# Splitting the last two weight blocks of fourteen more down products, and moving a product and eight squares near the end

## The chip, the cores and the metric

The kernel runs on one core of one Trainium2 chip. The metric is the device time of one execution in microseconds; of several runs the median is taken. The five engines that the profile names are PE (matrix products), DVE (vector), ACT (scalar), POOL and SP; SP here only issues DMAs.

## The reference

One layer of a hybrid encoder: a mixing part (attention, convolution and a two-way recurrent scan), then a mixture of sixteen experts, then a final normalisation. The change lies in the experts and in the end:

```python
def expert_choice_ffn(h, w_router, w_gate, w_up, w_down):
    B, S, D = h.shape                                  # 1, 1024, 1024
    cap = CAPACITY_FACTOR * S // N_EXPERTS             # 128 rows for each of 16 experts
    aff = jax.nn.softmax((h @ w_router).astype(jnp.float32), axis=-1)
    gates, idx = lax.top_k(jnp.swapaxes(aff, 1, 2), cap)
    xe = jax.vmap(lambda hb, ib: hb[ib])(h, idx)
    hid = jax.nn.silu(jnp.einsum('becd,edf->becf', xe, w_gate)) * jnp.einsum('becd,edf->becf', xe, w_up)
    ye = jnp.einsum('becf,efd->becd', hid, w_down) * gates[..., None].astype(h.dtype)
    bidx = jnp.arange(B)[:, None, None]
    return jnp.zeros_like(h).at[bidx, idx].add(ye)

    x = x + expert_choice_ffn(rms_norm(x, norm_ffn_g[l]), w_router[l], w_e_gate[l], ...)
    return rms_norm(x, final_norm_g)
```

All matrices are 1024x1024 float32, three for each expert: 192 MB of weights that are read once.

## The kernel before

The mixing part ends at about 860 us of the span; what follows is the experts' stage. An expert has three products: gate and up (from its 128 gathered rows `xe`) and down (from `hid`, the product of the two). Each is a sum over eight blocks of the contraction, `KT` = 8; a block is 128 rows of a weight matrix, and its product with the 128 rows fills two halves of 512 columns.

**How a block is computed.** A block is split: ACT rounds the raw float32 block into `ewh` (L1350 for down, L1354 for gate and up), DVE subtracts that from the raw block into `ewl` (L1351, L1355). The stationary side is split in the same way into `xh`, `xl` (rows) or `fh`, `fl` (hid). Then `mm3` makes three products for each half: high by high (L329), low by high (L330), high by low (L331), so six matmuls for a block. A block can also be left whole: `parts` yields the raw block with no low half, and `product` makes one float32 matmul for each half of it (L1455), with the whole stationary block `fw` (L1446). That is done for the last `NWHOLE` = 2 blocks of every down product, and for all eight of the last expert's (L1583).

**Buffers.** There are `NWB` = 5 pairs of `ewh` and `ewl`, so that at most five blocks lie split and not yet multiplied. Raw weights come in loads of 1 MB, two blocks each, into `NRAW` = 12 buffers (L1248, issued by SP in the order `order_w`); a load waits until its buffer's last reader is done.

**Order of the work.** In the code an expert's turn is: up of expert e, with the transposes of the next expert's rows behind its fourth block (`KTX`); on DVE `hid` times up (L1560); gate of expert e+1, with the gather of rows for e+2 behind its first block (`KTF`: one-hot products L1417, indices L1418, gather by POOL L1421) and the transposes of hid behind its third (`KTH`); down of expert e; then `add_back`: ACT scales the result into `ye` (L1482), POOL adds it to the rows of `x2_d` in memory by a scatter (L1483). The order in which each engine takes its instructions is set by a scheduler when the program is built; every engine then works in that order. A `ye` that waits for the down product therefore holds back all splits that stand behind it on ACT.

**The end.** Gate of expert 15 is broken: after `2 * BRK` = 4 of its blocks comes down of expert 14 (and its `add_back` and the loads of `last_loads`), then the other four. Up of expert 15 follows, the transposes of its hid, and its down product of whole blocks. Rows not in expert 15 are final once the scatter of expert 14 has landed: they are loaded (L1500), squared with a sum (L1514, ACT), multiplied by the final gain (L1516, DVE, five tiles of eight), scaled by the inverse root (L1520 on ACT, L1522 on DVE) and written (L1523). In `last_norm` the rows of expert 15 take the same steps and are written last by a scatter (L1537), which waits until the eight writes have landed.

Of the kernel before, what the change touches and what calls it, by code (L numbers as in the profile page):

```python
# [12 lines left out]
F32 = mybir.dt.float32  # L13
# [63 lines left out]
R_FIN = [-7, 21]  # L77
NRAW = 12
NWB = 5
BRK = 2  # L80

NGF = 5
NPRE = 2

NWHOLE = 2
NBOR = 0
PLACE = [11, 2, 3, 4, 5, 6, 7, 8, 1, 9, 10, 0]
NYE = 1
# [6 lines left out]
PF1 = 9  # L95

KTX, KTF, KTH = 3, 0, 2


@with_exitstack  # L100
def hybrid_block_kernel(ctx: ExitStack, tc: tile.TileContext, x, xT, memT, memn, w_in, w_mk, w_mv, pcols,
# [1236 lines left out]

    def parts():


        for i, (src, e, k2) in enumerate(order_w):
            raw = ahead.pop(i) if i in ahead else fetch_w(src, e, k2)
            for a in range(2):
                if src is w_ed and (e == NE - 1 or k2 * 2 + a >= KT - NWHOLE):
                    yield raw[a], None
                    continue
                h, l = halves.pop(0) if halves else [ex.tile([P, FF], F32R, name=n, bufs=NWB) for n in ("ewh", "ewl")]
                if src is w_ed:
                    A.activation(h, raw[a], AF.Copy)  # L1350
                    V.tensor_sub(l, raw[a], h.bitcast(F32))  # L1351
                else:
                    gain = col("g_ffn", 2 * k2 + a)
                    A.activation(h, raw[a], AF.Copy, scale=gain)  # L1354
                    V.scalar_tensor_tensor(l, raw[a], gain, h.bitcast(F32), op0=ALU.mult, op1=ALU.subtract)  # L1355
                yield h, l
# [70 lines left out]
                split.extend(next(parts) for _ in range(NWB))  # L1427
        return xe

    def transposed(src, nm, whole=0):  # L1430

        h = ex.tile([P, KT - whole, P], F32R, name=nm + "h", bufs=2 if nm == "x" else 1)
        l = ex.tile([P, KT - whole, P], F32R, name=nm + "l", bufs=2 if nm == "x" else 1)
        w = ex.tile([P, whole, P], F32, name=nm + "w", bufs=1) if whole else None
        for a in range(2):
            ps = mm("A", shape=[P, 4, P])
            for j in range(4):
                T.transpose(ps[:, j, :], src[:, (a * 4 + j) * P:(a * 4 + j + 1) * P], ident)  # L1438
            n = min(4, max(0, KT - whole - a * 4))
            s_ = slice(a * 4, a * 4 + n)  # L1440
            if n:
                A.activation(h[:, s_, :], ps[:, 0:n], AF.Copy)
                V.tensor_tensor(l[:, s_, :], ps[:, 0:n], h[:, s_, :].bitcast(F32), op=ALU.subtract)  # L1443
            if n < 4:
                i = a * 4 + n - (KT - whole)
                A.copy(w[:, i:i + 4 - n], ps[:, n:])  # L1446
        return h, l, w

    def product(acc, xh, xl, xw, then=None, ks=range(KT)):
        for k in ks:  # L1450
            h, l = split.pop(0) if split else next(parts)
            for n in range(2):
                sl = slice(n * 512, (n + 1) * 512)
                if l is None:
                    T.matmul(acc[n], lhsT=xw[:, k - KT + NWHOLE], rhs=h[:, sl], start=k == 0, stop=k == KT - 1)  # L1455
                else:
                    mm3(acc[n], xh[:, k, :], xl[:, k, :], h[:, sl], l[:, sl], k == 0, k == KT - 1)
            if then and k in then:
                for f in then[k]:
                    f()  # L1460
# [46 lines left out]
            out=last["own"], out_offset=None, in_=x2_d[:, :],  # L1507
            in_offset=bass.IndirectOffsetOnAxis(ap=idx[:, NE - 1:NE], axis=0)))

    def others():  # L1510

        junk = ex.tile([P, D], F32, name="fsq", tag="hid", bufs=2)
        for i, t in enumerate(last["x"]):
            A.activation(junk, t, AF.Square, accum_out=fs[:, i:i + 1])  # L1514
            if i < NGF:
                V.tensor_mul(t, t, last["g"])  # L1516
        rsqrt(fr[:, 0:NT], fs[:, 0:NT], 1.0 / D, NORM_EPS)
        for i, t in enumerate(last["x"]):
            if i < NGF:
                A.activation(t, t, AF.Copy, scale=fr[:, i:i + 1])  # L1520
            else:
                last["end"] = V.scalar_tensor_tensor(t, t, fr[:, i:i + 1], last["g"], op0=ALU.mult, op1=ALU.mult)  # L1522
            nc.sync.dma_start(out[i * P:(i + 1) * P, :], t)  # L1523
# [21 lines left out]
        xs[e] = transposed(rows.pop(e), "x")  # L1545

    def turn_h(e, done):
        hs[e] = transposed(done, "f", NWHOLE)

    def bring(e):  # L1550
        rows[e] = fetch(e)
# [2 lines left out]
    for e in range(NE):  # L1554
        up = [mm("y0"), mm("y1")]

        product(up, *xs.pop(e), {KTX: [lambda: turn_x(e + 1)]} if e + 1 < NE else None)
        for n in range(2):
            sl = slice(n * 512, (n + 1) * 512)
            V.scalar_tensor_tensor(hid[:, sl], up[n], gates[:, 1, e:e + 1], hid[:, sl], op0=ALU.mult, op1=ALU.mult)  # L1560
        done = hid
        if e + 1 < NE:
            then = {KTF: [lambda: bring(e + 2)] if e + 2 < NE else [], KTH: [lambda: turn_h(e, done)]}
            if e + 2 < NE:
                hid = gate(e + 1, xs[e + 1], then)
                add_back(e, hs.pop(e))
            else:
                hid = gate(e + 1, xs[e + 1], then, lambda: (add_back(e, hs.pop(e)), last_loads()))
        else:

            w = ex.tile([P, KT, P], F32, name="xh", bufs=2)
            for a, copy in enumerate((A.copy, V.tensor_copy)):
                ps = mm("A", shape=[P, 4, P])
                for j in range(4):
                    T.transpose(ps[:, j, :], done[:, (a * 4 + j) * P:(a * 4 + j + 1) * P], ident)
                copy(w[:, a * 4:(a + 1) * 4], ps)
            own_gather()
            others()
            dn = [mm() for _ in range(2)]
# [68 lines left out]
```

## Time and profile before

| | us |
|---|---|
| median of 3 runs | 1496.11 |
| lowest and highest of the 3 | 1487.31 and 1499.1 |
| the profiled execution | 1507.9 |
| its span, from first to last instruction | 1506.2 |

All rows come from the profiled execution, so sums are made against its 1507.9 us, of which 1.7 us lie outside of the span. It is 0.8% above the median; a difference found in it is carried to the median in that proportion.

### The profile page before, as it was taken

The numbers are of one execution on the slowest core, as the hardware profiler recorded it, in microseconds if no ns is written. First come the engines' busy times: TensorE is split into PE (matmuls) and PEld (weight loads), VectorE is DVE, ScalarE is ACT, GpSimd is POOL, SyncE is SP. The second block draws the span as 40 slices with busy tenths as digits, with TensorE's granted clock in tenths as the row PEclk, the third lists the DMA queues.
The fourth block names the chain that finished last, engine by engine and source line by source line (L and its number), as shares of the span: only waits on it lengthen the run. The fifth ranks groups of instructions, "written<-read, shape, count | busy, mean of one in ns | idle before, by whom it ended". The sixth has DMA issues, their size and how long they took to land.

```text
span 1506.2 us, 24148 instructions
## 1 busy us (share of the span) xinstructions
PE 1350.8 (90%) x9178; PEld 1063.8 (71%) x9178; DVE 1180.6 (78%) x2089; ACT 809.0 (54%) x1200; POOL 266.2 (18%) x238
## 2 busy tenths in 40 slices
PE   6888999997899888878999729999999999999995
PEld 4776657675777776667868628877777778877772
DVE  7899975699687869596833679988888888878875
ACT  4222574433535243433322418888787887767774
POOL 2233223432121212130221000000001101111000
PEclk9999999998889788887999859999999999999998
DMA  8222112412443433342473758999999999999975
GB/s 290 71 62 65 64 64 105 140 70 72 140 142 107 140 104 120 89 120 86 137 268 141 293 181 322 374 356 379 380 380 368 378 379 381 371 355 356 378 281 201
DMA packets 146100, 327.91 MB, mean 218 GB/s; under 512 B 9792, under 2 KB 64960, under 8 KB 145984
## 3 DMA queue, kind: packets, MB, share of 16 engines
q1 hardware_dynamic: 139360, 303.14, 54.9%
q0 software_dynamic: 6192, 22.55, 5.2%
q8 instruction: 72, 1.18, 0.3%
q10 hardware_dynamic: 432, 0.68, 0.1%
q14 instruction: 44, 0.36, 0.1%
HBM read 288.58 MB, written 37.75 MB: 217 GB/s over the span
## 4 chain that ended last, share of the span: by engine, by line
PE 62%; DVE 21%; ACT 5%; DMA 5%; issue 4%; POOL 1%; SPq 0%; POOLq 0%; ACTq 0%; DVEq 0%
PE mm L330 14%; PE mm L329 14%; PE mm L331 14%; PE mm L1455 3%; DVE cv L517 3%; DVE dtmp L910 2%; DVE Dt L911 2%; PE mm L1438 2%; DMA fo<-oT_d 2%; PE psA L854 1%; ACT Ld L895 1%; PE mm L745 1%; PE mm L1165 1%; PE psS L988 1%; DVE BK L826 1%
## 5 line engine op out<-in xcount | busy, mean ns | idle before, releaser
L1355 DVE SCALAR_TENSOR_TENSOR ewl<-eraw,pc,ewh 128x1024 fp32r<-128x1024 f32 x256 | 319.7, 1280 | 72.8 <-ACT ewh L1354 65.8
L1354 ACT ACTIVATE ewh<-eraw,pc 128x1024 fp32r<-128x1024 f32 x256 | 288.6, 1150 | 47.6 <-PE mm L331 46.2
L330 PE MATMUL mm<-ewl,xh 128*128 128x512 f32 x512 | 202.0, 394 | 1.7 <-DVE ewl L1355 1.6
L329 PE MATMUL mm<-ewh,xh 128*128 128x512 f32 x512 | 200.3, 409 | 1.0 <-ACT ewh L1354 1.0
L331 PE MATMUL mm<-ewh,xl 128*128 128x512 f32 x512 | 200.1, 391 | 0.0
L329 PE MATMUL mm<-hh,wh 128*128 128x512 f32 x304 | 127.0, 418 | 10.2 <-ACT hh L310 10.2
L330 PE MATMUL mm<-hl,wh 128*128 128x512 f32 x304 | 126.9, 417 | 0.2
L331 PE MATMUL mm<-hh,wl 128*128 128x512 f32 x304 | 126.2, 415 | 0.8 <-POOL wl L325 0.8
L330 PEld LDWEIGHTS mm<-ewl,xh 128*128 128x128 f32 x512 | 96.6, 189 | 26.1 <-DVE ewl L1355 5.2
L329 PEld LDWEIGHTS mm<-ewh,xh 128*128 128x128 f32 x512 | 96.3, 188 | 24.3 <-issue 4.1
L1351 DVE TENSOR_TENSOR ewl<-eraw,ewh 128x1024 fp32r<-128x1024 f32 x90 | 106.1, 1220 | 7.0 <-ACT ewh L1350 5.5
L331 PEld LDWEIGHTS mm<-ewh,xl 128*128 128x128 f32 x512 | 96.3, 188 | 20.0 <-DVE xl L1443 0.2
L1350 ACT ACTIVATE ewh<-eraw 128x1024 fp32r<-128x1024 f32 x90 | 92.5, 1058 | 10.8 <-PE mm L331 9.3
L1483 POOL DMA_INDIRECT x_d<-ye,idx x15 | 25.8, 1722 | 345.8 <-ACT ye L1482 345.8
L325 POOL TENSOR_TENSOR wl<-wraw,wh 128x512 fp32r<-128x512 f32 x38 | 57.9, 1527 | 129.2 <-ACT wh L324 111.4
L329 PEld LDWEIGHTS mm<-hh,wh 128*128 128x128 f32 x304 | 59.7, 196 | 26.5 <-ACT hh L310 10.7
L330 PEld LDWEIGHTS mm<-hl,wh 128*128 128x128 f32 x304 | 59.8, 197 | 18.0 <-DVE hl L311 2.9
L910 DVE TENSOR_TENSOR dtmp<-Lt,Dt 128x126 f32<-128x126 f32 (+22 forms) x186 | 70.5, 379 | 2.7
L517 DVE SCALAR_TENSOR_TENSOR cv<-u,cw,cv 128x512 f32<-128x512 f32 (+1 forms) x87 | 72.2, 860 | 0.1
L331 PEld LDWEIGHTS mm<-hh,wl 128*128 128x128 f32 x304 | 59.8, 197 | 16.3 <-POOL wl L325 3.2
L330 PE MATMUL mm<-ewl,fh 128*128 128x512 f32 x180 | 70.8, 393 | 0.1
L331 PE MATMUL mm<-ewh,fl 128*128 128x512 f32 x180 | 70.1, 389 | 0.0
(421 smaller groups left out, 2969.4 us busy)
## 6 DMA issues: line engine op xcount, KB each, us to landing
eraw<-in_w_eg_dram SPq DMA_DIRECT2D x64, 1024.0 KB, 10.2
eraw<-in_w_eu_dram SPq DMA_DIRECT2D x64, 1024.0 KB, 10.7
eraw<-in_w_ed_dram SPq DMA_DIRECT2D x64, 1024.0 KB, 8.1
fo<-oT_d SPq DMA_DIRECT2D x64, 320.0 KB, 3.9
wraw<-in_w_in_dram SPq DMA_DIRECT2D x38, 256.0 KB, 2.8
ld_k<-d_k SPq DMA_DIRECT2D x18, 256.0 KB, 3.3
ld_v<-d_v SPq DMA_DIRECT2D x18, 256.0 KB, 3.4
xk<-in_xT_dram SPq DMA_DIRECT2D x16, 256.0 KB, 4.9
```

What stands on the lines that cost most here:

```text
L325: G.tensor_sub(wl, raw, wh.bitcast(F32))
L329: T.matmul(ps, lhsT=lh, rhs=rh, start=first, stop=False)
L330: T.matmul(ps, lhsT=lh, rhs=rl, start=False, stop=False)
L331: T.matmul(ps, lhsT=ll, rhs=rh, start=False, stop=last)
L517: V.scalar_tensor_tensor(o[:, 0:ln], z, w, o[:, 0:ln], op0=ALU.mult, op1=ALU.add)
L910: IE.tensor_tensor(tmp[:, sg, ts], lcol, drow, op=ALU.mult)
L911: IE.tensor_tensor(Dt[:, sg, ts], Dt[:, sg, ts], tmp[:, sg, ts], op=ALU.add)
L1350: A.activation(h, raw[a], AF.Copy)
L1351: V.tensor_sub(l, raw[a], h.bitcast(F32))
L1354: A.activation(h, raw[a], AF.Copy, scale=gain)
L1355: V.scalar_tensor_tensor(l, raw[a], gain, h.bitcast(F32), op0=ALU.mult, op1=ALU.subtract)
L1455: T.matmul(acc[n], lhsT=xw[:, k - KT + NWHOLE], rhs=h[:, sl], start=k == 0, stop=k == KT - 1)
```

## The change

Three edits, and what they bring along:

- `NWHOLE` is gone: the down products of experts 0 to 14 split all eight blocks. `fh` and `fl` hold eight blocks, and `fw` with its copy is gone. Only the last expert's down product keeps whole blocks.
- `BRK` is 1: gate of expert 15 is broken after two blocks (one load) and no longer after four. The loads stand in the same order as the products: one load of gate 15, four of down 14, three of gate 15. The transposes of hid 14 are asked for behind gate block 0 there, and no longer behind block 2.
- The squares get a function of their own, called behind block 4 (`KTS`) of the last up product, and no longer behind the last transposes. The second of the two copies there moves from ACT to DVE.

```diff
-BRK = 2
+BRK = 1
-NWHOLE = 2
+KTS = 4
...
-                if src is w_ed and (e == NE - 1 or k2 * 2 + a >= KT - NWHOLE):
+                if src is w_ed and e == NE - 1:
                     yield raw[a], None
...
-        h = ex.tile([P, KT - whole, P], F32R, name=nm + "h", bufs=2 if nm == "x" else 1)
-        l = ex.tile([P, KT - whole, P], F32R, name=nm + "l", bufs=2 if nm == "x" else 1)
-        w = ex.tile([P, whole, P], F32, name=nm + "w", bufs=1) if whole else None
+        h = ex.tile([P, KT, P], F32R, name=nm + "h", bufs=2 if nm == "x" else 1)
+        l = ex.tile([P, KT, P], F32R, name=nm + "l", bufs=2 if nm == "x" else 1)
...
-                if l is None:
-                    T.matmul(acc[n], lhsT=xw[:, k - KT + NWHOLE], rhs=h[:, sl], start=k == 0, stop=k == KT - 1)
-                else:
-                    mm3(acc[n], xh[:, k, :], xl[:, k, :], h[:, sl], l[:, sl], k == 0, k == KT - 1)
+                mm3(acc[n], xh[:, k, :], xl[:, k, :], h[:, sl], l[:, sl], k == 0, k == KT - 1)
...
-    def others():
-
+    def squares():
         junk = ex.tile([P, D], F32, name="fsq", tag="hid", bufs=2)
         for i, t in enumerate(last["x"]):
             A.activation(junk, t, AF.Square, accum_out=fs[:, i:i + 1])
-            if i < NGF:
-                V.tensor_mul(t, t, last["g"])
+
+    def others():
+
+        for t in last["x"][:NGF]:
+            V.tensor_mul(t, t, last["g"])
...
-        product(up, *xs.pop(e), {KTX: [lambda: turn_x(e + 1)]} if e + 1 < NE else None)
+        product(up, *xs.pop(e), {KTX: [lambda: turn_x(e + 1)]} if e + 1 < NE else {KTS: [squares]})
...
-                hid = gate(e + 1, xs[e + 1], then, lambda: (add_back(e, hs.pop(e)), last_loads()))
+                hid = gate(e + 1, xs[e + 1], {0: [lambda: turn_h(e, done)]},
+                           lambda: (add_back(e, hs.pop(e)), last_loads()))
...
-            for a, copy in enumerate((A.copy, V.tensor_copy)):
+            for a in range(2):
...
-                copy(w[:, a * 4:(a + 1) * 4], ps)
+                V.tensor_copy(w[:, a * 4:(a + 1) * 4], ps)
```

The order of the instructions on an engine changes as follows. First ACT in the middle of the stage, one expert's turn (L1350 and L1349 are the splits of a down block, L1354 and L1353 those of gate and up); before:

```order
L1442 ACTIVATE fh<-mm 128x512
L1442 ACTIVATE fh<-mm 128x256
L1350 ACTIVATE ewh<-eraw 128x1024
L1446 COPY fw<-mm 128x256
L1350 ACTIVATE ewh<-eraw 128x1024 x3
L1470 ACTIVATE hid<-mm,gates 128x512 x2
L1350 ACTIVATE ewh<-eraw 128x1024 x2
L1354 ACTIVATE ewh<-eraw,pc 128x1024 x5
L1482 ACTIVATE ye<-mm,gates 128x512 x2
```

and after:

```order
L1437 ACTIVATE fh<-mm 128x512 x2
L1349 ACTIVATE ewh<-eraw 128x1024 x4
L1459 ACTIVATE hid<-mm,gates 128x512 x2
L1349 ACTIVATE ewh<-eraw 128x1024 x4
L1353 ACTIVATE ewh<-eraw,pc 128x1024 x4
L1471 ACTIVATE ye<-mm,gates 128x512 x2
```

Two more down blocks are split, and of the next product four blocks stand ahead of `ye` where there were five. This regular turn holds for experts 0 to 8 before and for experts 0 to 7 after.

Second ACT in the late experts, the end of expert 13's down product and the start of the next; before:

```order
L1350 ACTIVATE ewh<-eraw 128x1024 x2
L1354 ACTIVATE ewh<-eraw,pc 128x1024
L1482 ACTIVATE ye<-mm,gates 128x512
L1354 ACTIVATE ewh<-eraw,pc 128x1024
L1482 ACTIVATE ye<-mm,gates 128x512
L1354 ACTIVATE ewh<-eraw,pc 128x1024 x10
```

and after, the same place and on to `ye` of expert 14:

```order
L1353 ACTIVATE ewh<-eraw,pc 128x1024
L1471 ACTIVATE ye<-mm,gates 128x512 x2
L1353 ACTIVATE ewh<-eraw,pc 128x1024 x9
L1349 ACTIVATE ewh<-eraw 128x1024
L1437 ACTIVATE fh<-mm 128x512
L1349 ACTIVATE ewh<-eraw 128x1024
L1437 ACTIVATE fh<-mm 128x512
L1349 ACTIVATE ewh<-eraw 128x1024 x6
L1471 ACTIVATE ye<-mm,gates 128x512
```

Fewer splits of the next product stand ahead of the first half of `ye` here than in a regular turn: before four for expert 9, two for 10, one each for 11, 12 and 13 and none for 14; after, for experts 8 to 14, they are two, one, two, two, one, one and none. The splits for hid 14 (`fh`) come between the first down blocks of expert 14.

Third DVE at the end, from the last split to the first reciprocal root; before:

```order
L1355 SCALAR_TENSOR_TENSOR ewl<-eraw,pc,ewh 128x1024 x12
L1560 SCALAR_TENSOR_TENSOR hid<-mm,gates,hid 128x512 x2
L1576 COPY xh<-mm 128x512
L1516 TENSOR_TENSOR eraw<-eraw,gfi 128x1024 x5
L211 TENSOR_SCALAR rs_a<-fs 128x8
```

and after:

```order
L1354 SCALAR_TENSOR_TENSOR ewl<-eraw,pc,ewh 128x1024 x14
L1551 SCALAR_TENSOR_TENSOR hid<-mm,gates,hid 128x512 x2
L1568 COPY xh<-mm 128x512 x2
L1507 TENSOR_TENSOR eraw<-eraw,gfi 128x1024 x5
L211 TENSOR_SCALAR rs_a<-fs 128x8
```

Both copies are DVE's now, ahead of the five multiplications by the gain; on ACT the eight squares stand right behind the last split, with no copy between.

## Rows read from the trace of the kernel before

**Rows 1.** Page, part 1: busy us, share of the span, instructions, of each engine.

```profile
PE 1350.8 (90%) x9178; PEld 1063.8 (71%) x9178; DVE 1180.6 (78%) x2089; ACT 809.0 (54%) x1200; POOL 266.2 (18%) x238
```

**Rows 2.** Windows from one `ye` to the next: experts 5-6, 10-11, 11-12, 12-13.

```profile
core 0: us, PE busy (x) PEld busy (x) DVE busy (x) ACT busy (x) POOL busy (x), PEclk, DMA share, GB/s
1128.32:1164.42 36.10, 36.10 (x165) 28.84 (x164) 31.41 (x31) 29.01 (x31) 3.44 (x2) 1.00 1.00 378
1308.85:1347.59 38.74, 36.82 (x168) 28.87 (x167) 30.00 (x30) 26.31 (x30) 3.78 (x2) 1.00 0.98 368
1347.59:1385.81 38.22, 37.69 (x169) 28.99 (x168) 31.55 (x32) 27.76 (x32) 3.78 (x2) 1.00 0.96 357
1385.81:1423.13 37.32, 37.17 (x166) 28.62 (x165) 30.57 (x31) 27.89 (x32) 3.00 (x2) 1.00 0.97 362
```

**Rows 3.** Waits, 900 to 1400 us: us in total, times, longest.

```profile
ACT ewh L1354 <- PE mm L331: 46.2, 145, 1.7
...
DVE ewl L1355 <- DMA eraw<-in_w_ed_dram: 3.2, 1, 3.2
```

**Rows 4.** Timeline of PE: a split block's first matmul, the next block's; whole blocks.

```profile
1101.93 0.39 PE L329 MATMUL mm<-ewh,xh 128*128 128x512 f32 x1
...
1103.29 0.39 PE L329 MATMUL mm<-ewh,xh 128*128 128x512 f32 x1
...
1306.07 3.59 PE L1455 MATMUL mm<-eraw,fw 128*128 128x512 f32 x8
...
1309.74 0.40 PE L330 MATMUL mm<-ewl,xh 128*128 128x512 f32 x1
```

**Rows 5.** Groups of instructions by form, 900 to 1475 us: the splits of down blocks.

```profile
L1351 DVE TENSOR_TENSOR ewl<-eraw,ewh 128x1024 fp32r<-128x1024 f32 x90 | 106.1, 1220 | 7.0 <-ACT ewh L1350 5.5 <-DMA eraw<-in_w_eg_dram 0.3
L1350 ACT ACTIVATE ewh<-eraw 128x1024 fp32r<-128x1024 f32 x90 | 92.5, 1058 | 10.8 <-PE mm L331 9.3 <-DMA eraw<-in_w_eg_dram 0.3
...
L1443 DVE TENSOR_TENSOR fl<-mm,fh 128x512 fp32r<-128x512 f32 x15 | 10.4, 690 | 5.8 <-ACT fh L1442 5.8
...
L1443 DVE TENSOR_TENSOR fl<-mm,fh 128x256 fp32r<-128x256 f32 x15 | 6.2, 414 | 0.0
```

**Rows 6.** Timelines of ACT, DVE and PE: waits in the late experts.

```profile
1347.59 0.69 ACT L1482 ACTIVATE ye<-mm,gates 128x512 f32<-128x512 f32 x1 [5.55 <-PE mm L1455]
...
1349.35 1.28 DVE L1355 SCALAR_TENSOR_TENSOR ewl<-eraw,pc,ewh 128x1024 fp32r<-128x1024 f32 x1 [5.34 <-ACT ewh L1354]
...
1332.52 0.30 PE L1438 MATMUL mm<-ident,xe 128*128 128x128 f32 x1 [1.92 <-DMA xe<-h_d,idx]
...
1426.24 0.50 PE L330 MATMUL mm<-ewl,xh 128*128 128x512 f32 x1 [0.46 <-DVE ewl L1355]
...
1454.96 0.73 PE L329 MATMUL mm<-ewh,xh 128*128 128x512 f32 x2 [0.95 <-ACT ewh L1354]
1456.28 0.50 PE L330 MATMUL mm<-ewl,xh 128*128 128x512 f32 x1 [0.58 <-DVE ewl L1355]
```

**Rows 7.** Timelines of PE, ACT, DVE, SP, POOL: the end.

```profile
1474.81 14.00 PE L1583 MATMUL mm<-eraw,xh 128*128 128x512 f32 x32
...
1474.65 1.06 ACT L1514 ACTIVATE fsq<-eraw 128x1024 f32<-128x1024 f32 x1
...
1472.67 1.41 DVE L1560 SCALAR_TENSOR_TENSOR hid<-mm,gates,hid 128x512 f32<-128x512 f32 x2 [1.66 <-PE mm L331]
1474.83 0.69 DVE L1576 COPY xh<-mm 128x512 f32<-128x512 f32 x1 [0.75 <-PE mm L1575]
1475.83 5.95 DVE L1516 TENSOR_TENSOR eraw<-eraw,gfi 128x1024 f32<-128x1024 f32 x5 [0.31 <-ACT fsq L1514]
1484.10 0.17 DVE L211 TENSOR_SCALAR rs_a<-fs 128x8 f32<-128x8 f32 x1 [2.32 <-ACT fsq L1514]
...
1462.26 2.08 SPq L1500 DMA_DIRECT2D eraw<-x_d  x4
...
1500.23 0.97 POOL L1537 DMA_INDIRECT out_dram<-ye,idx  x1 [36.25 <-DMA out_dram<-eraw]
```

More of the change, by code (lines that the diff above doesn't have):

```diff
@@ L1428, in fetch, with transposed @@
         return xe
-    def transposed(src, nm, whole=0):
-        h = ex.tile([P, KT - whole, P], F32R, name=nm + "h", bufs=2 if nm == "x" else 1)
-        l = ex.tile([P, KT - whole, P], F32R, name=nm + "l", bufs=2 if nm == "x" else 1)
-        w = ex.tile([P, whole, P], F32, name=nm + "w", bufs=1) if whole else None
+    def transposed(src, nm):
+        h = ex.tile([P, KT, P], F32R, name=nm + "h", bufs=2 if nm == "x" else 1)
+        l = ex.tile([P, KT, P], F32R, name=nm + "l", bufs=2 if nm == "x" else 1)
         for a in range(2):
@@ L1438, in transposed, with product @@
                 T.transpose(ps[:, j, :], src[:, (a * 4 + j) * P:(a * 4 + j + 1) * P], ident)
[L1439 to L1449, printed above, removed]
+            s_ = slice(a * 4, (a + 1) * 4)
+            A.activation(h[:, s_, :], ps, AF.Copy)
+            V.tensor_tensor(l[:, s_, :], ps, h[:, s_, :].bitcast(F32), op=ALU.subtract)
+        return h, l
+    def product(acc, xh, xl, then=None, ks=range(KT)):
         for k in ks:
@@ L1547, in turn_h @@
     def turn_h(e, done):
-        hs[e] = transposed(done, "f", NWHOLE)
+        hs[e] = transposed(done, "f")
     def bring(e):
@@ L1562, in hybrid_block_kernel @@
         if e + 1 < NE:
-            then = {KTF: [lambda: bring(e + 2)] if e + 2 < NE else [], KTH: [lambda: turn_h(e, done)]}
             if e + 2 < NE:
+                then = {KTF: [lambda: bring(e + 2)], KTH: [lambda: turn_h(e, done)]}
                 hid = gate(e + 1, xs[e + 1], then)
```

## The prediction

> **What bounds the kernel now.** The page comes first: PE is busy for 90% of the span [rows 1], an average over stages that doesn't say what ends a wait. The windows of the experts' stage say it: from one `ye` to the next, in a regular turn of 36.10 us, PE is busy for all 36.10 at a granted clock of 1.00 (2.4 GHz), DVE for 31.41 and ACT for 29.01, and DMA shows a share of 1.00 [rows 2]. Two resources look full, and the waits tell them apart: ACT waits 145 times for PE to give back a split buffer, 46.2 us in all, while the longest wait of a split for its weights is 3.2 us, once in 500 us [rows 3]. So the loads are there in time and PE sets the pace. In the three turns from expert 10 to 13 the turn takes 38.74, 38.22 and 37.32 us: there PE waits now and then, and DVE and ACT stand behind a `ye` that waits for the down product [rows 2, 6].
>
> **The whole blocks.** From the first whole matmul at 1306.07 to an ordinary L330 at 1309.74 are 3.67 us, in which the L329 between takes an ordinary step; six such steps make a split block, 1101.93 to 1103.29 or 1.36 us, so a step is 0.227 [rows 4]. Two whole blocks take 3.67 - 0.23 = 3.44 us, two split ones 2 x 1.36 = 2.72, and the difference is 0.72. Fifteen experts make **-10.8 us** on an engine without idle time there. A regular turn becomes 36.10 - 0.72 = 35.38.
>
> What it adds elsewhere: for each expert two more splits, on ACT 2 x 1.06 and on DVE 2 x 1.22, and the second part of `fl` over four blocks and no longer two, 0.69 for 0.41 [rows 5]. (The copy `fw` that ACT loses I leave aside.) DVE comes to 31.41 + 2.44 + 0.28 = 34.13, ACT to 31.1. Both are under 35.38, so the cover is PE's own time; DVE keeps only 1.25 us of slack a turn. Where does DVE stand idle in a regular turn now? Mostly behind `ye`: ACT waits there for the down product, so that no new high half comes. With four blocks of the next product split ahead of `ye`, as the new order has it, PE has 4 x 1.36 = 5.4 us of work when down ends, and the first block behind `ye` follows some 3 us after (worked out below). So PE doesn't starve in the regular turns, and I take this part at nothing. If that cover is gone, see the first rival.
>
> DMA has to bring the same bytes in 35.38 us: 378 GB/s x 36.10 / 35.38 = 386. No row shows more over a turn, so the cost of that lies between nothing and the whole 0.72 a turn. I take nothing, because the splits don't wait for loads [rows 3] and twelve raw buffers are a whole turn of weights ahead.
>
> The Trainium skill ("DMA: Bandwidth & Descriptors", in "Where 436 GB/s comes from") says that for transfers between HBM and SBUF the HBM side binds at some 358 GB/s per core. By that this stage would already be at its end and the faster products would gain nothing. The trace has 378 GB/s over a whole turn [rows 2], above that figure, so I don't take it as the limit, but it is the third rival.
>
> **The late experts.** The order shows the regular turn until expert 7 now, and until expert 8 before, and fewer blocks split ahead of `ye` behind that. The price of such a `ye`: its two halves on ACT take 0.59 each (0.69 less the overlap), then a high half 1.06 and a low half 1.28, with some 0.1 between engines: 3.6 us from its start. It starts when the first half of the down product is done, half a block (0.68) ahead of down's end less about 0.2 of signalling, so the first new block is ready 3.1 us after down's end. With one block ahead PE has 1.36 us of work, and 0.45 in the first two matmuls of the next block, which need the high half alone: it waits 3.1 - 1.81 = 1.3. With two ahead it has 3.17 and waits for nothing. Experts 9 and 12 have one: 2.6 us. In the turn behind expert 8 the order also has the transposes of hid right behind the first two matmuls of a gate block. Hid times up takes 1.41 us on DVE [rows 7], then DVE still has that block to split (1.28), against 0.45 + 0.8 of work: 1.5 us. The gather wait of 1.92 us [rows 6] has a like in the same turn, with more time between gather and use; 0.5. Mixed orders cost about 0.1 at each change of tile (rows of 0.50 us beside the 0.39 and 0.40 [rows 4, 6]), some four a turn, five turns: 2.0. Sum 6.6. Before, three turns above 36.10 cost 2.64 + 2.12 + 1.22 = 5.98. Net **+0.6**. Bounds: if these waits all went, -6.0; if DVE is the pace there, the first rival.
>
> **Expert 13's `ye` to the last up product.** Behind expert 13 one block stands ahead now and before; the wait before was 0.46 [rows 6], and 1.3 by the sum above: +0.8. The transposes of hid 14 come two blocks earlier in gate 15. They need hid times up (1.41 and 0.2 of signalling) right behind up 14, then `fh`, `fl` and the first down splits, and DVE has 1.28 + 0.69 + 1.22 queued ahead of what PE wants; PE has 1.36 + 0.45 of cover: about +1.2. The `ye` of expert 14 has no split ahead of it in the new order: PE waits for 0.13 + 1.06 + 0.1 + 1.28 = 2.5 us, less 0.45, so 2.05, and 0.2 at the next block, against 0.95 + 0.58 before [rows 6]: +0.7. Together **+2.7**, between 0 and +4.
>
> **The end.** Before, ACT begins the eight squares at 1474.65, behind a copy that waits for the transposes, and the first root at 1484.10 waits 2.32 us for the last square; DVE's five multiplications wait 0.31 for the first [rows 7]. In the new order the squares stand behind the last split; DVE's part of that was done at 1472.67 - 1.66 = 1471.01, ACT's before. What is late next? The loads of the rows: issued at 1462.26 when the scatter of expert 14 has landed [rows 7]. With down 14 two blocks (2.7 us) earlier they move ahead too, so I take all squares to be done before DVE has gone through hid, two copies (the second, 0.69, was DVE's already; the first is new, but the last product needs only it to start, as before) and five multiplications. Then DVE goes straight into the roots: 2.32 + 0.31 = **-2.6**. The eight writes follow the root, and the last scatter waits for them, 36.25 us in all [rows 7], so the gain reaches the end. Bounds: -2.6, since DVE's own list is no shorter, and 0 if the loads are late or the last rows' own chain behind the product that ends at 1488.81 becomes the last.
>
> **Sum.** -10.8 + 0.6 + 2.7 - 2.6 = -10.1 us. The profiled execution takes 1507.9, so 1497.8; its share of the median is 0.9922, which gives **1486.1**, or 0.7% faster. Half of the late turns' 6.6 us to either side, and the bounds of the two terms behind it (not all at once), make 1481 to 1492 the forecast's own range.
>
> **Rivals.** *DVE sets the pace in the late experts* (the one that ends slower). A late `ye` kept DVE idle for 5.34 us [rows 6]; with 34.13 of work the turn is 39.5 and not 36.7. Five such turns add 14 us: -10.1 + 14 = +4, 1500. For it: DVE has 2.72 us more to do and the late turns begin two experts earlier. Against: once PE waits, DVE works through and its idle time shrinks. It decides from an idle time of some 4.6 us a turn, where the late turns have taken back the whole gain (10.1 / 5 = 2.0 a turn above 36.7). Chance 0.13.
>
> *The late waits vanish* with the whole blocks, on which `ye` had to wait: -10.8 - 6.0 - 1.5 - 2.6 = -20.9, 1475. For it: the scheduler's order is new in every late turn. Against: it has fewer splits ahead of `ye` in more turns. Chance 0.13.
>
> *DMA keeps the turns at 36.10*: the 10.8 is not to be had, +0.7, 1497. For it: the share of 1.00. Against: no wait for weights. Chance 0.08.
>
> *The squares don't move*, though the diff calls them earlier: the order still has them behind the last split, and if the loads are late too the end gives nothing: 1488.7. It lies within the forecast.
>
> **How the numbers follow.** Forecast 0.62, rivals 0.13, 0.13 and 0.08; the rest, 0.04, for something that isn't in the profile. The bound that a measurement can tell is 1%, 15 us. Faster by over 1%, under 1481: the second rival and a part of the forecast's lower end, 0.21. Slower by over 1%: 0.04. Within: 0.75. The range takes the forecast, the DMA rival, and the near halves of the others: 1477 to 1498.
>
> **What would show it.** No L1455 groups, and the regular turns at 35.4 with PE busy throughout: the first term. DVE idle under 1.3 us in them. Late turns between 35.8 and 37.8: the second; 39 or more, and DVE busy throughout: the first rival. Waits of splits for loads of several us: the third. The first root's wait for the squares gone, and the last write earlier against the last product by 2.6 us: the end. The prediction is wrong above all if DVE, with 1.25 us of slack a turn, can't stay ahead of PE.

## The result, and the profile after

The changed kernel takes 1487.37 us, median of 20 runs (1477.59 to 1494.88), where the kernel before took 1498.34 beside it (20 runs, 1487.03 to 1513.53): a ratio of 0.9932, 95% interval 0.991 to 0.9954. The slowest of the 20 executions of before is in a slower state and is left out of the ratio. The forecast was 1486.1 us, 0.9933 of the 1496.11 that it started from. (The 0.9922 in its sum is the share that carries the profiled execution over to the median, and no ratio of the kernels.)

The first part of the page of after (columns as in [rows 1]):

```profile
PE 1333.4 (90%) x9238; PEld 1069.4 (72%) x9238; DVE 1216.1 (82%) x2120; ACT 831.2 (56%) x1214; POOL 266.4 (18%) x238
```

PE is busy for 17.4 us less and DVE for 35.5 us more. The two profiled spans, 1506.2 and 1487.2 us, differ by 19 us, but 8.3 of these lie ahead of the first expert matmul (at 900.48 and 892.20), in work that the change doesn't touch. So all that follows is read from that matmul on. Windows of before, then of after (columns as in [rows 2]): from it to the last product's start, and from there to the end.

```profile
900.48:1474.81 574.33, 569.23 (x2558) 449.68 (x2557) 484.64 (x476) 442.30 (x482) 52.48 (x31) 1.00 0.97 362
1474.81:1506.15 31.34, 14.00 (x32) 5.99 (x32) 16.99 (x37) 15.56 (x25) 0.97 (x1) 0.79 0.40 159
```

```profile
892.20:1458.92 566.72, 559.74 (x2618) 460.28 (x2617) 519.62 (x508) 470.25 (x506) 53.40 (x31) 1.00 0.99 367
...
1116.17:1151.56 35.39, 35.39 (x170) 29.60 (x169) 33.69 (x34) 30.62 (x34) 3.44 (x2) 1.00 1.03 390
...
1221.93:1261.10 39.17, 38.19 (x183) 30.55 (x182) 33.26 (x34) 29.39 (x34) 3.37 (x2) 1.00 0.98 347
1261.10:1298.58 37.48, 36.60 (x172) 29.73 (x171) 35.39 (x37) 30.39 (x34) 5.65 (x3) 1.00 0.98 365
1298.58:1334.46 35.88, 35.79 (x169) 29.38 (x168) 33.56 (x34) 29.13 (x32) 3.40 (x2) 1.00 1.02 385
...
1370.35:1406.63 36.28, 35.12 (x161) 28.47 (x160) 32.20 (x30) 29.13 (x33) 1.59 (x1) 1.00 1.01 366
1406.63:1434.47 27.84, 26.38 (x116) 20.59 (x115) 22.63 (x21) 19.41 (x22) 1.57 (x1) 1.00 1.01 377
1434.47:1458.92 24.45, 22.12 (x96) 16.50 (x94) 19.16 (x18) 22.94 (x29) 3.73 (x2) 1.00 0.70 239
1458.92:1487.17 28.25, 14.00 (x32) 5.99 (x32) 16.71 (x37) 9.88 (x15) 0.97 (x1) 0.83 0.42 167
```

The stage is 7.6 us shorter and the end 3.1, together 10.7 us. In the stage PE is busy for 9.5 us less, and its idle time (first number less the second) grows from 5.1 to 7.0. A regular turn takes 35.39 us where it took 36.10 [rows 2], with PE busy throughout. The late turns, two experts earlier than before, take 39.17 to 35.88. The five from `ye` 8 to `ye` 13 in one window:

```profile
1221.93:1406.63 184.70, 181.50 (x850) 147.56 (x849) 166.95 (x165) 146.01 (x162) 17.39 (x10) 1.00 1.00 367
```

PE is idle for 3.2 us there.

Waits from 892 to 1392 us of after (columns as in [rows 3]):

```profile
ACT ewh L1353 <- PE mm L331: 25.7, 85, 1.7
...
ACT ewh L1349 <- PE mm L331: 9.5, 32, 0.3
...
ACT ewh L1353 <- DMA eraw<-in_w_eu_dram: 3.5, 8, 1.1
ACT ewh L1353 <- DMA eraw<-in_w_ed_dram: 1.2, 5, 0.3
```

Splits still wait for PE's buffers (35.2 us), and for loads 4.7 us in 13 pieces, none longer than 1.1. DMA moved 390 GB/s over the turn and PE didn't wait for it.

PE's waits behind the `ye` of experts 8 (two), 9, 12, 13 and 14, from its timeline (columns as in [rows 6]):

```profile
1237.76 0.50 PE L330 MATMUL mm<-ewl,xh 128*128 128x512 f32 x1 [0.54 <-DVE ewl L1354]
...
1242.57 0.95 PE L1435 MATMUL mm<-ident,xe 128*128 128x128 f32 x7 [0.44 <-DVE ewl L1354]
...
1264.95 0.50 PE L330 MATMUL mm<-ewl,xh 128*128 128x512 f32 x1 [0.66 <-DVE ewl L1354]
...
1372.70 0.74 PE L329 MATMUL mm<-ewh,xh 128*128 128x512 f32 x2 [0.58 <-ACT ewh L1353]
1374.02 0.50 PE L330 MATMUL mm<-ewl,xh 128*128 128x512 f32 x1 [0.58 <-DVE ewl L1354]
...
1408.98 0.73 PE L329 MATMUL mm<-ewh,xh 128*128 128x512 f32 x2 [0.58 <-ACT ewh L1353]
1410.31 0.50 PE L330 MATMUL mm<-ewl,xh 128*128 128x512 f32 x1 [0.59 <-DVE ewl L1354]
...
1436.24 0.74 PE L329 MATMUL mm<-ewh,xh 128*128 128x512 f32 x2 [1.13 <-ACT ewh L1353]
1437.56 0.50 PE L330 MATMUL mm<-ewl,xh 128*128 128x512 f32 x1 [0.58 <-DVE ewl L1354]
```

And the end, timelines of ACT, DVE, SP and POOL, which answer to [rows 7]:

```profile
1452.81 1.05 ACT L1502 ACTIVATE fsq<-eraw 128x1024 f32<-128x1024 f32 x1
...
1458.17 1.35 DVE L1568 COPY xh<-mm 128x512 f32<-128x512 f32 x2
1459.44 5.76 DVE L1507 TENSOR_TENSOR eraw<-eraw,gfi 128x1024 f32<-128x1024 f32 x5
1465.11 0.16 DVE L211 TENSOR_SCALAR rs_a<-fs 128x8 f32<-128x8 f32 x1
...
1443.43 2.06 SPq L1489 DMA_DIRECT2D eraw<-x_d  x4
...
1481.25 0.97 POOL L1528 DMA_INDIRECT out_dram<-ye,idx  x1 [35.27 <-DMA out_dram<-eraw]
```

The squares begin 6.1 us ahead of the last product; the loads of their rows were issued 15.5 us ahead of it, and before 12.5. The root follows the multiplications without a wait: 6.19 us behind the product's start, and before it was 9.29.

### The profile page after: what moved, and what is told of

Its sections match the earlier page's. It is cut to its first block, busy times and chain, and to the rows that moved or that the text cites. A ratio compares the mean times of both kernels' runs of the same rounds, so it can differ in the third digit from the quotient of the medians.

```text
span 1487.2 us, 24329 instructions
## 1 busy us (share of the span) xinstructions
PE 1333.4 (90%) x9238; PEld 1069.4 (72%) x9238; DVE 1216.1 (82%) x2120; ACT 831.2 (56%) x1214; POOL 266.4 (18%) x238
## 4 chain that ended last, share of the span: by engine, by line
PE 60%; DVE 23%; DMA 6%; ACT 5%; issue 4%; POOL 1%; SPq 0%; POOLq 0%; DVEq 0%; ACTq 0%
PE mm L330 14%; PE mm L331 14%; PE mm L329 14%; DVE cv L517 3%; DVE dtmp L910 2%; DVE Dt L911 2%; DMA fo<-oT_d 2%; PE mm L1435 2%; ACT Ld L895 2%; DMA xk<-in_xT_dram 1%; PE mm L745 1%; PE psA L854 1%; DVE ewl L1354 1%; PE mm L1165 1%; PE mm L1575 1%
## 5 line engine op out<-in xcount | busy, mean ns | idle before, releaser
L1354 DVE SCALAR_TENSOR_TENSOR ewl<-eraw,pc,ewh 128x1024 fp32r<-128x1024 f32 x256 | 315.6, 1280 | 30.5 <-ACT ewh L1353 28.4
L1353 ACT ACTIVATE ewh<-eraw,pc 128x1024 fp32r<-128x1024 f32 x256 | 283.8, 1149 | 31.7 <-PE mm L331 25.7
L329 PE MATMUL mm<-ewh,xh 128*128 128x512 f32 x512 | 190.4, 397 | 2.5 <-ACT ewh L1353 2.5
L1350 DVE TENSOR_TENSOR ewl<-eraw,ewh 128x1024 fp32r<-128x1024 f32 x120 | 139.0, 1219 | 2.8 <-ACT ewh L1349 2.8
L1349 ACT ACTIVATE ewh<-eraw 128x1024 fp32r<-128x1024 f32 x120 | 121.6, 1057 | 10.6 <-PE mm L331 9.5
L330 PE MATMUL mm<-ewl,fh 128*128 128x512 f32 x240 | 94.6, 394 | 0.3 <-DVE ewl L1350 0.2
L331 PE MATMUL mm<-ewh,fl 128*128 128x512 f32 x240 | 93.6, 390 | 0.0
L329 PE MATMUL mm<-ewh,fh 128*128 128x512 f32 x240 | 88.0, 390 | 0.0
L1472 POOL DMA_INDIRECT x_d<-ye,idx x15 | 25.9, 1724 | 283.3 <-ACT ye L1471 283.3
L1420 POOL DMA_INDIRECT xe<-h_d,idx x16 | 28.9, 1805 | 247.0 <-DVE gates L1418 182.3
L330 PEld LDWEIGHTS mm<-hl,wh 128*128 128x128 f32 x304 | 59.1, 194 | 17.4 <-issue 2.7
```

What stands on the lines that cost most here:

```text
L329: T.matmul(ps, lhsT=lh, rhs=rh, start=first, stop=False)
L330: T.matmul(ps, lhsT=lh, rhs=rl, start=False, stop=False)
L331: T.matmul(ps, lhsT=ll, rhs=rh, start=False, stop=last)
```

## The experiments

This table has each profiled execution in four stretches (us): from the first expert matmul to `ye` 0, on to `ye` 8, to `ye` 13, to the last product's start (as "break"), and the end; then their sum without the end, and the ratio to the kernel before.

| kernel | to ye 0 | to ye 8 | to ye 13 | break | end | stage | ratio (95%) |
|---|---|---|---|---|---|---|---|
| before | 47.3 | 288.8 | 186.5 | 51.7 | 31.3 | 574.3 | |
| after | 47.1 | 282.6 | 184.7 | 52.3 | 28.3 | 566.7 | 0.9932 (0.991 to 0.9954) |
| split alone | 47.2 | 282.6 | 185.0 | 54.9 | 31.4 | 569.7 | 0.9977 (0.995 to 1.0003) |
| break alone | 47.4 | 288.8 | 186.5 | 52.2 | 31.3 | 574.9 | 1.0009 (0.9985 to 1.0033) |
| squares and copies | 47.1 | 288.8 | 186.4 | 51.8 | 28.2 | 574.1 | 0.999 (0.9961 to 1.002) |
| two extra on DVE | 48.2 | 289.7 | 193.4 | 51.4 | 28.2 | 582.6 | 1.0044 (1.0011 to 1.0077) |
| split and break | 47.2 | 282.6 | 184.6 | 52.2 | 31.4 | 566.6 | 0.9957 (0.9926 to 0.9987) |
| split alone, filled | 47.1 | 282.6 | 185.3 | 52.2 | 31.4 | 567.1 | 0.9967 (0.9939 to 0.9996) |
| blocks in line | 47.1 | 282.6 | 184.8 | 52.0 | 28.3 | 566.5 | 0.9932 (0.9905 to 0.996) |
| all in line | 53.0 | 283.3 | 177.1 | 47.5 | 28.3 | 560.9 | 0.9907 (0.9871 to 0.9942) |
| start mended | 49.9 | 283.4 | 177.1 | 47.5 | 28.3 | 557.9 | 0.9879 (0.9847 to 0.991) |

The ratios resolve some 3 us at best; a stretch whose instructions stand in the same order repeats within 0.7 us (`ye` 8 to `ye` 13 of after, split alone, split and break and filled: 184.6 to 185.3), most within 0.3. So parts of a few us are told apart by the stretches, and the ratios only confirm the sums.

**The split alone.** The kernel before with one number changed.

```diff
-NWHOLE = 2
+NWHOLE = 0
```

> The kernel before with its split rule alone changed: no block of a down product stays whole except those of the last one; the break, the squares and the copies stay as before. Theory 1 (matmul time of the whole blocks, less late waits): a regular turn of 35.4 us where it was 36.1, the stage from the first expert matmul to the last product's start 15 x 0.72 = 10.8 us shorter less 1 to 2 us of late waits, so 565 us where it was 574.3, the end after that start unchanged at 31 us; ratio about 0.994, some 9 us faster. Rival (the vector engine or the transfers pay it back): turns at 36.1 and a ratio of 1.000. Rival (the break is what lets the gain through): the stretch from the ye of expert 13 to the last product's start grows by the 3 us or more that the changed kernel avoids, ratio above 0.996.

Seven turns of 35.4 us and one of 35.0, as the first theory has them; but the stage came out 4.7 us shorter, not 9. The second rival is right: the stretch behind `ye` 13 grew by 3.3 us, though its matmuls had become 0.7 us cheaper. PE's timeline there, then windows of 4 us:

```profile
1442.99 0.80 PE L329 MATMUL mm<-ewh,xh 128*128 128x512 f32 x2 [1.94 <-ACT ewh L1354]
1444.31 0.80 PE L330 MATMUL mm<-ewl,xh 128*128 128x512 f32 x1 [0.52 <-DVE ewl L1355]
1444.90 0.63 PE L331 MATMUL mm<-ewh,xl 128*128 128x512 f32 x1
```

```profile
1440.00:1444.00 4.00, 1.84 (x7) 0.84 (x5) 1.03 (x1) 3.37 (x5) 1.56 (x1) 0.94 0.00 0
1444.00:1448.00 4.00, 3.69 (x9) 2.92 (x10) 4.00 (x5) 4.00 (x4) 0.00 (x0) 0.50 0.87 131
1448.00:1452.00 4.00, 4.00 (x14) 3.19 (x13) 2.23 (x2) 0.36 (x2) 2.08 (x1) 0.71 0.68 196
1452.00:1456.00 4.00, 4.00 (x18) 3.04 (x17) 1.79 (x2) 4.00 (x5) 0.00 (x0) 1.00 1.02 419
```

Down of expert 14 ends, its `ye` has no split ahead of it, and PE waits 1.94 and 0.52 us. The granted clock is then 0.50 (1.2 GHz) from 1444 to 1448, and the windows of 0.50 and 0.71 hold 9 and 14 matmuls where the next one holds 18. So a wait of 2.5 us is followed by a loss of about its own size.

**The break alone.** The turning of hid 14 moves along, ahead of the break.

```diff
-BRK = 2
+BRK = 1
...
-            then = {KTF: [lambda: bring(e + 2)] if e + 2 < NE else [], KTH: [lambda: turn_h(e, done)]}
+            then = {**({KTF: [lambda: bring(e + 2)]} if e + 2 < NE else {}), (KTH if e + 2 < NE else 0): [lambda: turn_h(e, done)]}
```

> The kernel before with the break alone changed: down of expert 14 breaks into gate 15 after two blocks, not four, and the turning of hid 14 comes after the first block of the gate. Whole blocks, squares and copies as before. Theory 1 (the break costs two waits, for hid 14 and for ye 14): the stretch from the ye of expert 13 to the last product's start 1 to 3 us longer than 51.7, all else the same; ratio 1.000 to 1.002, no difference that can be measured. Rival (the earlier break serves the end, its loads start sooner): the end after the last product's start 2 us or more shorter than 31.3, ratio 0.998.

The stretch is 0.5 us longer, the end the same: alone the break gives nothing, and costs less than the 1 to 3 us expected.

**The squares and the copies alone.**

```diff
+    def squares():
         junk = ex.tile([P, D], F32, name="fsq", tag="hid", bufs=2)
         for i, t in enumerate(last["x"]):
             A.activation(junk, t, AF.Square, accum_out=fs[:, i:i + 1])
-            if i < NGF:
-                V.tensor_mul(t, t, last["g"])
+
+    def others():
+
+        for t in last["x"][:NGF]:
+            V.tensor_mul(t, t, last["g"])
...
-        product(up, *xs.pop(e), {KTX: [lambda: turn_x(e + 1)]} if e + 1 < NE else None)
+        product(up, *xs.pop(e), {KTX: [lambda: turn_x(e + 1)]} if e + 1 < NE else {4: [squares]})
...
-            for a, copy in enumerate((A.copy, V.tensor_copy)):
+            for a, copy in enumerate((V.tensor_copy, V.tensor_copy)):
```

> The kernel before with the squares and the copies alone changed: the squares of the other rows stand after block 4 of the last up product, and the vector engine copies both halves of the turned hid 15. Whole blocks and break as before. Theory 1 (the squares were what the roots waited for): the roots no longer wait the 2.3 us for the squares, the end after the last product's start 28 to 29 us where it was 31.3, the stage unchanged; ratio 0.998. Rival (the squares only move, or the rows land too late for them without the earlier break): the roots still wait for the squares and the end stays at 31 us, ratio 1.000. Rival (the squares hold up the splits of gate 15's or up 15's last blocks): the last product starts 1 to 8 us later, ratio above 1.001.

The end is 28.2 us, all of the changed kernel's 3.1, with the break still at two loads' blocks; the stage is the same within 0.2. The ratio alone could not have said so. On ACT three of the squares wait for their rows here (1.67, 0.40 and 0.19 us), but the last is done at 1466.5, 0.7 us ahead of the root. DVE's timeline of this kernel, in which the last product starts at 1461.01:

```profile
1460.26 1.35 DVE L1578 COPY xh<-mm 128x512 f32<-128x512 f32 x2
1461.53 5.76 DVE L1518 TENSOR_TENSOR eraw<-eraw,gfi 128x1024 f32<-128x1024 f32 x5
1467.20 0.17 DVE L211 TENSOR_SCALAR rs_a<-fs 128x8 f32<-128x8 f32 x1
```

Which of the two edits does it? Built with the copies alone, the program has the order of this one on every engine; with the squares alone, that of the kernel before (neither was timed). In the order of the kernel before, the squares stand on ACT behind its copy, and that waits for the transposes of hid 15; calling them earlier in the text doesn't move them. It is the copy's leaving ACT that lets them go. (The copy that leaves is the first of the two, and not the second as the list of edits has it: the second was DVE's already.)

**Two extra subtractions on DVE in each down product,** put on the changed kernel.

```diff
                     V.tensor_sub(l, raw[a], h.bitcast(F32))
+                    if a == 1 and k2 >= 2:
+                        V.tensor_sub(l, raw[a], h.bitcast(F32))
```

> The changed kernel with two subtractions of each down product's splits done twice on the vector engine (same result): 2 x 1.16 us more of its work in each turn. Theory 1 (the matmuls set the turn, the vector engine has 0.8 to 1.7 us of slack in it): the slack is used up, a regular turn 36.0 to 36.6 us where it is 35.4, in all 10 to 18 us slower than the changed kernel, which is about the time of the kernel before or a few us above. Rival (the vector engine sets the turn already): a turn 2.3 us longer, 37.7, some 33 us slower. Rival (ample slack on the vector engine): turns stay at 35.4.

A regular turn takes 36.2 us, within the first theory's bounds, and the kernel 1503.31 us, 16 above the changed one. Windows of it, a regular turn and a late one:

```profile
1006.40:1042.61 36.21, 35.87 (x169) 29.26 (x168) 35.74 (x36) 30.27 (x33) 4.48 (x2) 1.00 1.01 377
...
1332.51:1374.04 41.53, 38.03 (x170) 30.35 (x169) 36.92 (x37) 30.04 (x33) 4.38 (x2) 0.96 0.91 330
```

DVE is busy for 35.74 of 36.21 and PE now waits for it in each turn (0.3 us before a gather's matmuls). So the slack was real: DVE's busy time grew by 2.05 us (33.69 to 35.74), its idle time fell from 1.70 to 0.47, so that 1.2 us of slack were used, and the turn became 0.8 longer. Of the 16 us only 7.0 come from the eight turns to `ye` 8 and 8.7 from the five behind it, where two turns took 41.5 and 43.1, with waits of 2.96 and 5.01 us for gathered rows, and the clock fell to 0.57 after both. That the whole lies within the theory's 10 to 18 us is therefore in part chance.

**The split and the break together** (squares and copies as before; the diff is the first two put together).

> The split rule and the break together; squares and copies as before. The split alone gave 4.7 us in the stage, since after down of expert 14 the matmul engine waited 1.94 and 0.52 us and the granted clock then stood at 0.50 for some 5 us. Theory (the earlier break keeps that wait short, so that the clock stays up): after ye 14 waits near 1.1 and 0.6 us, clock 1.00, the stretch from ye 13 to the last product's start 52.3 us where the split alone has 54.9; stage 566.7, end 31.3; ratio 0.995. Rival (the clock fell there by chance of that one execution): the stretch within 0.5 us of 54.9 or the same fall of the clock here. Rival (the squares and the copies are what keeps it): 54.9 here too.

The waits are 1.14 and 0.58 us, the clock 1.00, the stretch 52.2 and the stage 566.6. What the break does is seen in ACT's order around the `ye` of expert 14, first in the split alone, then in the changed kernel, whose order there is that of split and break:

```profile
1440.63 1.27 ACT L1482 ACTIVATE ye<-mm,gates 128x512 f32<-128x512 f32 x2 [5.29 <-PE mm L331]
1441.79 6.34 ACT L1354 ACTIVATE ewh<-eraw,pc 128x1024 fp32r<-128x1024 f32 x6
```

```profile
1434.47 0.69 ACT L1471 ACTIVATE ye<-mm,gates 128x512 f32<-128x512 f32 x1 [5.06 <-PE mm L331]
1435.05 1.14 ACT L1353 ACTIVATE ewh<-eraw,pc 128x1024 fp32r<-128x1024 f32 x1
1436.09 0.68 ACT L1471 ACTIVATE ye<-mm,gates 128x512 f32<-128x512 f32 x1
```

In the split alone both halves of `ye` stand ahead of the first split, which starts 1.16 us behind the first half; in the changed kernel one split stands between them and starts 0.58 behind it. So the parts don't add: the split alone gives 4.7 us, the break alone takes 0.6, and both give 7.7.

**The split alone, with the wait filled.**

```diff
-                hid = gate(e + 1, xs[e + 1], then, lambda: (add_back(e, hs.pop(e)), last_loads()))
+                hid = gate(e + 1, xs[e + 1], then, lambda: (add_back(e, hs.pop(e)), fill(12), last_loads()))
...
+    def fill(count):
+        ps = mm("A", shape=[P, 4, P])
+        for j in range(count):
+            tc.keep_in_program_order(T.transpose(ps[:, j % 4, :], ident, ident))
```

> The split alone, with 12 transposes of the unit matrix into a spare PSUM tile put on the matmul engine behind the last matmul of down 14; nothing reads them. They take 12 x 0.16 = 1.9 us and lie in the wait that follows. Theory (the wait lets the clock fall): the wait shrinks to under 0.3 us, the granted clock stays 1.00, and the stretch from ye 13 to the last product's start is 52.3 to 52.8 us where it was 54.9. Rival (the clock falls for another reason, or what is slow there is not the clock): 54.9 again.

PE's timeline and the window from `ye` 14 to the last product:

```profile
1437.45 1.47 PE L1506 MATMUL mm<-ident 128*128 128x128 f32 x12
1439.56 0.73 PE L329 MATMUL mm<-ewh,xh 128*128 128x512 f32 x2 [0.63 <-ACT ewh L1354]
1440.88 0.50 PE L330 MATMUL mm<-ewl,xh 128*128 128x512 f32 x1 [0.59 <-DVE ewl L1355]
```

```profile
1437.20:1459.02 21.82, 20.19 (x94) 15.48 (x92) 15.94 (x14) 15.77 (x18) 3.52 (x2) 1.00 0.71 241
```

The transposes took 1.5 us and not 1.9, and left a wait of 0.63. They do nothing for the result and PE still goes on only when the split is there, yet the window takes 21.82 us where it took 24.64: 2.8 us, which is what the clock cost in that execution.

Each of these traces is one execution, so they alone don't refute that the clock fell by chance, and the ratios (0.9977 and 0.9967) are too near to each other. But every execution's mean granted clock is on record: its mean is 0.922 in the 12 of the split alone, where the kernel before, timed beside it, had 0.927, and the break alone and the squares and copies 0.926; later split and break had 0.925, filled 0.927, and the kernel before, beside these, 0.925. So the lower clock of the split alone is not that of one execution. (The difference of 0.005 is more than 5 us at half the clock would make, some 0.002; what else is in it I have not traced.)

**The blocks in line.** The changed kernel with each block's first matmul behind the block written before it, in issue order only.

```diff
-                mm3(acc[n], xh[:, k, :], xl[:, k, :], h[:, sl], l[:, sl], k == 0, k == KT - 1)
+                before_ = order_pe[-1] if order_pe else None
+                i0 = len(order_pe)
...
+                    tc.add_manual_dep(order_pe[i0].ins, before_.ins.name,
```

> The changed kernel with the matmul blocks of the products held in the order in which they are written (each block's first matmul behind the last one's last, in issue order only); transposes, gathers and the other engines stay where the planner puts them. Theory (mixing blocks in experts 8 to 13 costs the matmul engine its waits): the five turns from ye 8 to ye 13 lose 2 to 4 of their 7.8 us over five regular turns. Rival (the place of the transposes and with it the order on the scalar and the vector engine makes the waits): the stage from the first expert matmul to the last product's start within 1.5 us of 566.7.

566.5 us: nothing, and from `ye` 8 to `ye` 13 184.8 with PE busy for 181.2, as in the changed kernel. My theory that mixed blocks cost the late experts their time falls; the rival stands.

**All in line.** PE, ACT and DVE in program order over the whole stage; each block, once issued, asks for the split five blocks on; the one-hot of expert e + 3 is made in down of e.

```diff
+    fixed = tc.manual_schedule(engines={mybir.EngineType.PE, mybir.EngineType.Activation, mybir.EngineType.DVE})
+    fixed.__enter__()
...
-            h, l = split.pop(0) if split else next(parts)
+            h, l = split.pop(0)
...
+            if not (wait and k == KT - 1):
+                split.extend(islice(parts, 1))
...
-        dn = down(e, hs)
+        dn = down(e, hs, {3: [lambda: hot(e + 3)]} if e + 3 < NE else None)
```

> The changed kernel with the matmul, scalar and vector engines held in program order over the whole experts' stage, splits written five blocks ahead of their use, the one-hot of expert e + 3 in down of e, so that the late experts and the stretch at the break have the order of a regular turn. Theory (the late experts' excess is order, not the vector engine or the transfers): all turns 35.4 us, ye 8 to ye 13 in 177 us where it was 184.7, ye 13 to the last product's start 49 to 51 us, stage 556 to 560, some 7 to 10 us faster than the changed kernel, 1478 to 1481. Rival (from expert 8 on the transfers fall behind, the lead of the loads being used up): late turns stay above 36.5 and the waits go over to DMA; within 3 us of the changed kernel. Rival (program order makes the engines wait for each other in each turn): regular turns above 35.6, slower than the changed kernel.

Windows of it: the first stretch, `ye` 13 to 14, on to the last product, and `ye` 0 to `ye` 13.

```profile
888.82:941.77 52.95, 50.30 (x223) 41.42 (x223) 44.74 (x43) 41.14 (x42) 0.94 (x1) 0.95 0.84 297
1402.21:1430.13 27.92, 27.07 (x126) 21.75 (x125) 25.55 (x25) 23.01 (x26) 1.59 (x1) 1.00 0.92 342
1430.13:1449.68 19.55, 19.26 (x89) 15.36 (x87) 14.46 (x15) 17.05 (x23) 3.59 (x2) 1.00 0.72 239
...
941.77:1402.21 460.44, 460.44 (x2186) 384.39 (x2185) 438.18 (x429) 397.82 (x418) 47.93 (x26) 1.00 1.02 386
```

Every one of the thirteen turns takes 35.4 us and PE doesn't wait once in 460 us. DVE does 33.7 us a turn, DMA 386 GB/s, as in the changed kernel's regular turns: neither was the late experts' limit. At the break, ACT's timeline has the fifth split of gate 15 ahead of the `ye` of expert 14:

```profile
1429.07 1.15 ACT L1354 ACTIVATE ewh<-eraw,pc 128x1024 fp32r<-128x1024 f32 x1 [0.21 <-PE mm L331]
1430.13 1.25 ACT L1481 ACTIVATE ye<-mm,gates 128x512 f32<-128x512 f32 x2
1431.27 4.39 ACT L1354 ACTIVATE ewh<-eraw,pc 128x1024 fp32r<-128x1024 f32 x4
```

so PE goes on there without a wait, and the stretch from that `ye` is 19.55 us. The stage, 560.9, is just outside of the 556 to 560 expected. The first stretch lost 5.8 us: PE waited 2.65 us for the one-hot of expert 2, and the granted clock was 0.75 and 0.83 in the two windows of 4 us behind that.

**The start mended.** That one-hot is made ahead of the first gate.

```diff
-        if e == 0:
-            on[6] = [lambda: hot(2)]
...
+    hot(2)
     fixed = tc.manual_schedule(engines={mybir.EngineType.PE, mybir.EngineType.Activation, mybir.EngineType.DVE})
```

> The kernel with all three engines in line, with the one-hot of expert 2 made ahead of the first gate, no longer in its up product, where the matmul engine waited 2.65 us for it and the granted clock then fell. Theory (that wait and the fall made the first stretch, from the first expert matmul to ye 0, 52.95 us where the changed kernel has 47.1): 47 to 47.5 us now, the rest as it was; stage 555 to 555.6, some 11 us below the changed kernel's 566.7, end 28.3; about 1475, ratio 0.985. Rival (program order itself makes the start slow, the splits of the first gate being late): the first stretch stays above 50 us.

The first stretch is 49.9, between the theory's 47.5 and the rival's 50: 3.0 of the 5.8 us are back, and 2.8 are not. Of these, 1.25 are a wait at the turning of hid 0, and 1.36 are no loss: in this order one block more is multiplied ahead of `ye` 0 (50 high-by-high matmuls of gate and up, and not 48), and the last stretch has one block less. The forecast left that block out. The stage is 8.8 us shorter than the changed kernel's, and 1479.96 us with a ratio of 0.9879 is the lowest of these kernels, though not told apart from all in line. It and the changed kernel were not timed together; by their ratios to the kernel before it is some 0.5% ahead, with intervals that touch at 0.991.

## Why the prediction was right, and where its steps were off

- **Whole blocks, -10.8.** Right to the hundredth in a turn: 35.38 forecast, 35.39 measured, and the split alone gives the same turns.
- **DVE at nothing, with 1.25 us of slack.** Right: 33.7 us of work in a turn (34.13 forecast), and with the extra subtractions the turn grew once some 1.2 us of slack were used.
- **DMA at nothing.** Right: 390 GB/s in a regular turn, and no wait of a split for loads over 1.1 us. The rival that kept the turns at 36.10 is out. The Trainium skill ("HBM Reference", in "Specifications (TRN2)") says that a core streaming alone gets well above the share of 358 GB/s, some 425; the trace agrees as far as it goes, 386 GB/s over 460 us.
- **The late experts, +0.6.** They cost 7.8 us over five regular turns, 0.4 of which the turn ahead, 35.00, gave: 7.4 where the forecast had 6.6, so +1.4. The size was near, the parts were not. PE's idle time is 3.2 us: the forecast's 1.3, 1.3, 1.5 and 0.5 came out as 0.87 (0.21 and 0.66), 1.17, 0.54 and 0.44 (the last put down to a split and not to the gather), and 0.2 stand elsewhere. (The high half behind a late `ye` is one of gate or up and takes 1.15, and not the 1.06 of the forecast.) The other 4.6 us lie in rows that count as busy. Eight more transposes than five regular turns have, at 0.10 each, are 0.8 of them; the rest is not explained. A row lasts 0.39 us and the next starts 0.227 behind it [rows 4], so a wait under some 0.16 us leaves no idle time, but that these are such waits is not shown. The forecast had 2.0 for mixed blocks there, and the blocks in line refute it. All in line, the same stretch takes 177.1, so the 7.6 us are the order's on the three engines; which of its edits brings that is not separated.
- **Behind `ye` 13, +2.7.** It came out at +1.3: 52.29 us against 51.68 less 0.72. Behind `ye` 13 the waits are 1.17 for 0.46, as forecast (+0.8). The step that failed is hid 14, put at +1.2: its transposes found hid ready, and no wait stands there, only 0.20 and 0.10 at the first low halves of down 14. (All in line, PE waits 0.50 us for hid 14 and 0.34 for its low half: such a price exists, but the scheduler's order didn't ask it.) Behind `ye` 14 the waits are 1.71 for 1.53, +0.2 where I had +0.7.
- **The break as a mere price.** I counted its waits and left out what they do to the clock. Without it the split alone loses 2.7 us more (54.95 for 52.29), so in this kernel the break pays for itself.
- **The end, -2.6.** It gave 3.1: the two waits of 2.32 and 0.31, 0.2 because the multiplications took 5.76 for 5.95, 0.2 because the copies end earlier against the product, and 0.1 because the root starts that much ahead of the last multiplication's end. I counted on the earlier break to bring the rows in time for the squares; it isn't needed, since the squares and copies alone give the same end. And what moved the squares is the copy's going to DVE, not the earlier call.
- **DVE as the pace of the late experts** (the slower rival) is out: all in line, DVE does the same work in late turns of 35.4. **The late waits vanish** didn't happen here, but all in line shows that it could have, for some 11 us with the break's stretch (7.6, and 4.8 less the block of 1.4 that stands ahead of `ye` 0 there).

The sum of the terms was -10.1 and the trace gives -10.7: the late experts cost 0.8 more than forecast, the break 1.4 less, the end gave 0.5 more, and the first stretch, to `ye` 0, gave 0.2 of the 0.7 that its whole blocks promised. That last one is mostly where the stretch is cut: before, `ye` 0 starts with one of its eight whole-block rows (0.43 us) still to come, and the last stretch has nine. Taken together the two stretches, first and last, changed by +0.4 where the forecast had +1.3. So the forecast's mechanism holds for the whole blocks and for the roots' wait, but that the sum fits within 0.6 us is in part luck: the errors of +0.8, -1.4, -0.5 and +0.5 cancel in part.

## What to carry to other kernels

Price a matmul change where its engine has no idle time: there it came out exactly. The order that a scheduler writes around it was worth as much again here, and is found by comparing late turns with regular ones. A wait of the matmul engine costs its length and then, if the granted clock falls, more (2.8 us behind waits of 2.5 in the split alone, 1.6 behind 2.65 in all in line, by the mended start): look at the clock of the windows behind each wait, and don't add up parts that share one. An instruction that is called earlier in the text need not move on its engine: look at the order that was built, and for what stands in front of it there.

## What the runs showed that I had not expected

The granted clock fell after quite short waits: after 1.94 and 0.52 us with two matmuls between (split alone, 0.50 from 1444 to 1448), after 2.65 (all in line, 0.75 and 0.83), after 2.96 and 5.01 (two extra on DVE, 0.57). It stayed at 1.00 after 1.13 and 0.58 (after), after 1.14 and 0.58 (split and break), and in the kernel before after a single 1.92 [rows 2, 6]. The Trainium skill ("TensorE: Matmul & The Clock Gate", in "HAM oscillation — how this bites in real kernels") tells of kernels whose waits put the array back to its lower clock; these rows agree, and filling the wait with idle transposes gave 2.8 us back.

One execution's stage ahead of the experts differs from another's by up to 15 us (first expert matmul at 885.9 to 900.5 us in these profiles), though the experts' stage repeats within some tenths. I take most of the scatter of the whole times to come from there; no run shows it. What the record does show is that the longer executions are those with the lower mean granted clock: of the changed kernel's 20 the fastest, 1477.59 us, has 0.937, and the slowest, 1494.88, has 0.921.
